# Dividing a softmax by its sums on ScalarE in place of GpSimd, in one attention stage of a two-layer decoder

## The chip, the cores and the metric

The kernel runs on one core of a Trainium2 chip. The metric is the device time of one execution in microseconds (us); the time of a kernel is the median of several runs. The engines are TensorE (PE in the profile; PEld is its loading of weights), VectorE (DVE), ScalarE (ACT), GpSimd (POOL) and SyncE (SP), which issues the DMAs.

## The reference

Two decoder layers work on 512 tokens of 1024 numbers in float32. Each layer is a SwiGLU feed-forward half-step, an attention and another half-step, all behind an RMS norm. The first layer's attention is "stick-breaking", the second's is sliding-window attention with 16 query heads of 64 and 2 key heads, and it is there that the change lies. Its softmax has one more term in the denominator, a learned "sink" of each head:

```python
m = jnp.maximum(jnp.max(scores, axis=-1, keepdims=True), sink)
p = jnp.exp(scores - m)
probs = p / (jnp.sum(p, axis=-1, keepdims=True) + jnp.exp(sink - m))
o = jnp.einsum('bnkgts,bnskd->bntkgd', probs.astype(v_band.dtype), v_band)
```

A block of 128 queries sees its own 128 keys and the 128 before it, behind a band mask; the first block has only its own.

## The kernel before

The program is a chain of stages: a feed-forward stage, the first attention, two feed-forward stages, the second attention (`sliding_window`, L1141) and a last feed-forward stage. Float32 products are made of three faster ones: a weight or an operand is split into a high half (a cast on ScalarE, in L345 for weights) and a low half (a subtraction, L350 on VectorE or L348 on GpSimd), and TensorE multiplies high by high, high by low and low by high (`terms`, L214).

TensorE's instructions keep the order in which the program issues them (class `_Ordered`, L75). ScalarE, VectorE (outside the first part of a feed-forward stage) and GpSimd get their order from the scheduler of the framework, which fills each engine's queue when the kernel is built, by priority and by when it reckons that an instruction can start; on the chip each queue is then worked off in that order. Semaphores are set by the framework from the tiles that an instruction reads and writes.

The second attention is cut into 16 turns: 4 chunks `c` of 4 heads, and in each 4 blocks `b` of 128 queries. In turn u (the loop of L1172) three things are interleaved:

- `window_scores` (L1045) of this turn: TensorE makes the scores `sc` of 4 heads (L1054 to L1059). VectorE adds the band mask and takes the row maxima in one instruction a head (L1067) and forms the shift of the exponent from the maxima and the sinks in three small ones (L1071 to L1073). This is the first part; in the next turn, ScalarE takes the exponent with the row sums, one Exp a head (L1076), and that of the sinks (L1080); VectorE adds the two (L1082) and takes the reciprocal (L1083); and GpSimd multiplies the whole tile `e` by the reciprocals, four heads in one instruction (L1084). A tile `e` is 128 x 4 x 256, in the first block of a chunk 128 x 4 x 128, and there are 4 buffers of it.
- `window_values` (L1088) of a turn three back: TensorE transposes `e` (`ptr`, L1100), ScalarE casts the result to a high half `ph` (L1103), VectorE subtracts to a low half `pl` (L1104), and TensorE multiplies both with the values (`pv`, L1112). ScalarE and VectorE split the product in the same way (`oh` L1113, `ol` L1114). The transposes have two PSUM buffers, shared with those of the queries (`qtr`, L1040), so a transpose waits until an earlier `ph` and `pl` have read theirs.
- Filling work for TensorE, a number of microseconds of it after each step (the lists WFILL and WRATE, L43 and L44): the products of the next chunk's queries (`tok`) and, later, those of the output matrix (`op`). The queries are squared on ScalarE (`qsq`, L1029), scaled on VectorE (L1030), given their rotary turn on GpSimd (L958 to L961), normalised on VectorE (`head_factor`, L963), transposed, and split by L644 on ScalarE and L645 on VectorE (`qs`).

The steps of a turn, cut to what matters:

```python
late = turning.pop(0) if u > 2 and turning else None
if scores:
    next(scores)               # the Exps of the turn before
...
if scores:
    next(scores)               # its sums, reciprocals and L1084
...
    scores = self.window_scores(c, b, turned[c], qs[c][0], e)
    turning.append(self.window_values(c, b, e, os, parts))
```

So a tile is normalised in the turn after its scores and transposed three turns after them.

Of the kernel before, what the change touches and what calls it, by code (L numbers as in the profile page):

```python
# [11 lines left out]
AF = mybir.ActivationFunctionType  # L12
# [3 lines left out]
P = 128  # L16
# [171 lines left out]
class _Trunk:  # L188
# [856 lines left out]
    def window_scores(self, c, b, qt, y, out):  # L1045

        nc, ap = self.nc, self.ap
        kh, kl = self.kt[c // 2]
        off = 0 if b else P
        ks = slice(max(b - 1, 0) * P, (b + 1) * P)  # L1050
        ts = slice(b * P, (b + 1) * P)
        z = self.psum.tile([P, 2, T], F32, tag="z", name="sc", bufs=1)
        z4 = z.rearrange("p q (i s) -> p q i s", i=2)
        for i in range(2):  # L1054
            for q in range(2):
                self.mm(z4[:, q, i, off:], qt[i][:, q, ts], kh[:, ks], start=True, stop=False)
            for q in range(2):
                rows = slice(q * HD, (q + 1) * HD)
                self.mm(z4[:, q, i, off:], qt[i][rows, q, ts], kl[rows, ks], start=False, stop=True)  # L1059
        yield  # L1060
        e = ap.tile([P, 4, 2 * P], F32, tag="e", name="e", bufs=4)
        st = ap.tile([P, 4, LINE // 4], F32, tag="st", name="st", bufs=4)[:, :, :4]
        f = y[:, 4 * b : 4 * b + 4]
        sink = self.sinks[:, 4 * c : 4 * c + 4]
        mx, neg, es, sm = (st[:, n, :] for n in range(4))
        for h in range(4):
            nc.vector.tensor_tensor_reduce(  # L1067
                e[:, h, off:], z4[:, h % 2, h // 2, off:], self.band[:, off:],
                scale=1.0, scalar=NEG, op0=ALU.add, op1=ALU.max, accum_out=mx[:, h : h + 1],
            )  # L1070
        nc.vector.scalar_tensor_tensor(mx, mx, -1.0, f, ALU.mult, ALU.mult)  # L1071
        nc.vector.scalar_tensor_tensor(neg, sink, -1.0, mx, ALU.mult, ALU.min)
        nc.vector.tensor_add(es, sink, neg)  # L1073
        yield
        for h in range(4):
            nc.scalar.activation(  # L1076
                e[:, h, off:], e[:, h, off:], AF.Exp, bias=neg[:, h : h + 1], scale=f[:, h : h + 1],
                accum_out=sm[:, h : h + 1],
            )
        nc.scalar.activation(es, es, AF.Exp)  # L1080
        yield
        nc.vector.tensor_add(sm, sm, es)  # L1082
        nc.vector.reciprocal(sm, sm)  # L1083
        nc.gpsimd.tensor_mul(e[:, :, off:], e[:, :, off:], sm[:, :, None].broadcast_to([P, 4, 2 * P - off]))  # L1084
        out.append(e)
        yield

# [223 lines left out]
```

## Time and profile before

| | us |
|---|---|
| median of 3 runs (1879.17 to 1884.75) | 1881.69 |
| the profiled execution's own time | 1884.44 |
| its span, first to last instruction | 1882.6 |
| TensorE busy (97% of the span) | 1834.2 |
| VectorE busy (80%) | 1500.1 |
| ScalarE busy (50%) | 938.1 |
| GpSimd busy (9%) | 170.2 |

The mean granted clock of TensorE over the execution is 0.985 of 2.4 GHz. The second attention lies at about 1340 to 1510 us of the span, its 16 turns at 1380 to 1503. In a timeline a row gives start, duration, engine, line, operation, output and inputs, shapes and count; in brackets stands how long the engine was idle before and what ended that. The line L85 is a helper's through which TensorE's instructions pass; it is told apart by the names of the tiles. "Granted clock" is the share of full speed at which TensorE was let run.

### The profile page before, as it was taken

The page shows a single profiled execution, that of the slowest core. Times are in us where ns is not written, and L with a number is a line of the kernel's source. Part 1 is how long each engine was busy: PE and PEld are TensorE (multiplying, and loading weights), DVE is VectorE, ACT ScalarE, POOL GpSimd, SP SyncE. Part 2 cuts the span into 40 slices and gives each one's busy share as a digit, 9 for nine tenths or more (in the row PEclk, how much of TensorE's full clock was granted, in tenths as well). Part 3 has the DMA queues.
Part 4 walks back from the last instruction along what each step waited for, and adds up shares of the span by engine and source line. Part 5 has one row for each costly group of instructions (what it writes and reads, how often), then busy time and mean ns, then how long its engine had stood idle before and what let it go on. Part 6 is the DMA issues. An engine that isn't in the chain of part 4 may idle for free.

```text
span 1882.6 us, 29285 instructions
## 1 busy us (share of the span) xinstructions
PE 1834.2 (97%) x11730; PEld 1651.1 (88%) x11730; DVE 1500.1 (80%) x2426; ACT 938.1 (50%) x1497; POOL 170.2 (9%) x131
## 2 busy tenths in 40 slices
PE   7999999999999999999999999999999899999999
PEld 5999999878787789999988999999887788999998
DVE  8888888668886988878768888787678588888884
ACT  6444444465664644444446444444356564444441
POOL 1000000333230100000010000000242210000000
PEclk8999999999999999999999999999989899999999
DMA  4333333221121423333323323322211043233331
GB/s 168 101 101 101 101 104 99 69 78 57 57 68 34 134 83 98 105 109 97 106 68 123 101 90 105 119 88 92 73 58 33 12 134 101 95 108 101 102 101 57
DMA packets 48809, 170.95 MB, mean 91 GB/s; under 512 B 5792, under 2 KB 6048, under 8 KB 48672
## 3 DMA queue, kind: packets, MB, share of 16 engines
q1 hardware_dynamic: 48672, 169.07, 28.2%
q8 instruction: 92, 1.51, 0.3%
q14 instruction: 45, 0.37, 0.1%
HBM read 166.96 MB, written 2.10 MB: 90 GB/s over the span
## 4 chain that ended last, share of the span: by engine, by line
PE 80%; DVE 11%; ACT 4%; issue 3%; POOL 1%; DMA 0%; SPq 0%; ACTq 0%; DVEq 0%; POOLq 0%
PE dn L85 25%; PE a L85 23%; PE c L85 11%; PE b L85 6%; PE gu L85 4%; PE tok L85 3%; PE op L85 3%; DVE keep L732 2%; PE pv L85 1%; DVE beta L733 1%; DVE t L85 1%; DVE qs L645 1%; PE sc L85 1%; DVE wt L755 1%; ACT keep L726 1%
## 5 line engine op out<-in xcount | busy, mean ns | idle before, releaser
L85 PE MATMUL dn<-hs,slot 128*128 128x512 f32 x1152 | 279.1, 391 | 0.0
L85 PEld LDWEIGHTS dn<-hs,slot 128*128 128x128 f32 x1152 | 211.0, 188 | 40.4
L85 PE MATMUL dn<-hs,slotx 128*128 128x512 f32 x960 | 234.2, 392 | 2.2 <-DVE hs L85 1.3
L345 ACT CAST slot<-raw 128x1024 fp32r<-128x1024 f32 (+1 forms) x155 | 160.0, 1033 | 145.1 <-PE a L85 55.2
L85 PE MATMUL a<-t,slot 128*128 128x256 f32 x1728 | 230.2, 283 | 0.0
L85 PEld LDWEIGHTS a<-t,slot 128*128 128x128 f32 x1728 | 222.7, 191 | 6.6
L85 PEld LDWEIGHTS dn<-hs,slotx 128*128 128x128 f32 x960 | 175.4, 188 | 37.5 <-DVE hs L85 2.2
L474 DVE SCALAR_TENSOR_TENSOR x<-dn,x 128x512 f32<-128x512 f32 x192 | 131.5, 685 | 44.9 <-PE dn L85 44.8
L350 DVE TENSOR_TENSOR slot<-raw,slot 128x1024 fp32r<-128x1024 f32 (+1 forms) x117 | 143.8, 1231 | 9.9 <-ACT slot L345 9.9
L85 PEld LDWEIGHTS a<-t,slotx 128*128 128x128 f32 x1008 | 131.0, 191 | 5.3
L85 PE MATMUL a<-t,slotx 128*128 128x256 f32 x1008 | 134.1, 283 | 0.0
L348 POOL TENSOR_TENSOR slot<-raw,slot 128x512 fp32r<-128x512 f32 x60 | 87.6, 1485 | 477.4 <-ACT slot L345 473.4
L85 PE MATMUL b<-xh,half 128*128 128x256 f32 x608 | 121.8, 283 | 0.0
L441 POOL TENSOR_TENSOR acc<-acc,sq 128x512 f32<-128x512 f32 x30 | 44.3, 1476 | 804.3 <-ACT sq L440 804.3
L85 PE MATMUL tok<-slot,xh 128*128 128x256 f32 x576 | 113.6, 296 | 0.1
L85 PEld LDWEIGHTS b<-xh,half 128*128 128x128 f32 x608 | 100.3, 192 | 0.0
L345 ACT CAST slotx<-raw 128x1024 fp32r<-128x1024 f32 x64 | 66.8, 1050 | 66.4 <-PE a L85 56.7
L345 ACT CAST slot<-rawx 128x1024 fp32r<-128x1024 f32 x60 | 63.1, 1052 | 69.7 <-PE a L85 43.6
L85 PE MATMUL c<-xh,slot 128*128 128x256 f32 x480 | 96.2, 283 | 0.0
L85 PEld LDWEIGHTS tok<-slot,xh 128*128 128x128 f32 x576 | 92.2, 197 | 3.3 <-issue 1.3
L553 DVE TENSOR_TENSOR g<-c,r 128x256 f32<-128x256 f32 x76 | 32.2, 424 | 75.8 <-PE c L85 75.6
L85 PE MATMUL gu<-xh,slot 128*128 128x512 f32 x256 | 87.3, 412 | 3.8 <-ACT xh L432 1.7
(360 smaller groups left out, 4216.7 us busy)
## 6 DMA issues: line engine op xcount, KB each, us to landing
raw<-in_w_dram SPq DMA_DIRECT2D x165, 512.0 KB, 3.5
rawx<-in_w_dram SPq DMA_DIRECT2D x96, 512.0 KB, 3.5
raw<-in_sbqk_dram SPq DMA_DIRECT2D x16, 512.0 KB, 3.4
raw<-in_swin_dram SPq DMA_DIRECT2D x10, 512.0 KB, 3.5
raw<-in_sbv_dram SPq DMA_DIRECT2D x8, 512.0 KB, 3.4
raw<-in_sbo_dram SPq DMA_DIRECT2D x8, 512.0 KB, 3.4
raw<-in_swo_dram SPq DMA_DIRECT2D x8, 512.0 KB, 3.4
x<-in_xt_dram SPq DMA_DIRECT2D x8, 256.0 KB, 5.4
```

The costliest lines, as they stand in the source:

```text
L85: return self._tc.keep_in_program_order(method(*args, **kwargs))
L345: nc.scalar.copy(hi, src)
L348: nc.gpsimd.tensor_sub(lo[:, h], src[:, h], hi[:, h])
L350: nc.vector.tensor_sub(lo, src, hi)
L441: (nc.gpsimd if k < POOL_SQUARES else nc.vector).tensor_add(self.acc, self.acc, sq)
L474: self.nc.vector.scalar_tensor_tensor(self.x[n], ps, factor, self.x[n], ALU.mult, ALU.add)
L553: nc.vector.tensor_add(g[:, W2:], ps, self.cells["r6", f])
L645: nc.vector.tensor_sub(out[other, h, :], src[own, :], out[own, h, :])
L726: nc.scalar.activation(keep[:, :, :n], z[:, :, :n], AF.Sigmoid, scale=-0.125)
L732: nc.vector.tensor_tensor_scan(rev, rev, rev, 1.0, ALU.mult, ALU.bypass)
L733: nc.vector.tensor_mul(beta[:, :, : n - 1], beta[:, :, : n - 1], keep[:, :, 1:n])
L755: nc.vector.tensor_sub(lo, src, hi)
```

## The change

The one instruction on GpSimd that multiplies the whole tile `e` by its four columns of reciprocals is replaced by four on ScalarE, one a head, each a Copy with the head's column as its scale. Result and place in the program stay the same. The diff in full:

```diff
@@ -1081,7 +1081,8 @@
         yield
         nc.vector.tensor_add(sm, sm, es)
         nc.vector.reciprocal(sm, sm)
-        nc.gpsimd.tensor_mul(e[:, :, off:], e[:, :, off:], sm[:, :, None].broadcast_to([P, 4, 2 * P - off]))
+        for h in range(4):
+            nc.scalar.activation(e[:, h, off:], e[:, h, off:], AF.Copy, scale=sm[:, h : h + 1])
         out.append(e)
         yield
```

## Rows read from the trace of the kernel before

**Rows 1.** The page's head and its part on busy time.

```profile
span 1882.6 us, 29285 instructions
PE 1834.2 (97%) x11730; PEld 1651.1 (88%) x11730; DVE 1500.1 (80%) x2426; ACT 938.1 (50%) x1497; POOL 170.2 (9%) x131
```

**Rows 2.** Windows: length; PE, PEld, DVE, ACT, POOL busy; PE's granted clock; DMA.

```profile
1380.00:1503.00 123.00, 109.26 (x697) 94.44 (x696) 91.24 (x322) 76.21 (x216) 41.03 (x34) 0.92 0.10 31
1464.00:1470.00 6.00, 5.86 (x23) 5.10 (x24) 3.24 (x16) 3.72 (x14) 1.89 (x1) 0.50 0.01 3
1483.00:1488.00 5.00, 4.02 (x15) 3.62 (x16) 3.38 (x17) 4.58 (x17) 1.77 (x2) 0.66 0.01 3
```

**Rows 3.** Timeline of TensorE, second attention: what it did after six waits.

```profile
1405.28 0.82 PE L85 MATMUL ptr<-ident,e 128*128 128x128 f32 x4 [1.95 <-DVE pl L1104]
...
1435.52 0.66 PE L85 MATMUL ptr<-ident,e 128*128 128x128 f32 x4 [1.55 <-DVE pl L1104]
...
1441.54 0.38 PE L85 MATMUL pv<-pl,v 128*128 128x256 f32 x1 [0.83 <-DVE pl L1104]
...
1457.47 0.66 PE L85 MATMUL qtr<-ident,q 128*128 128x128 f32 x4 [1.61 <-DVE pl L1104]
...
1464.14 1.12 PE L85 MATMUL ptr<-ident,e 128*128 128x128 f32 x4 [3.48 <-DVE pl L1104]
...
1483.98 0.46 PE L85 MATMUL pv<-pl,v 128*128 128x256 f32 x1 [1.34 <-DVE pl L1104]
```

**Rows 4.** Timeline of VectorE, second attention.

```profile
1401.18 0.17 DVE L1083 RECIPROCAL st<-st 128x4 f32<-128x4 f32 x1
...
1431.91 1.51 DVE L1071 SCALAR_TENSOR_TENSOR st<-st,hf 128x4 f32<-128x4 f32 x1
...
1438.31 2.57 DVE L350 TENSOR_TENSOR slot<-raw,slot 128x1024 fp32r<-128x1024 f32 x1
...
1441.40 1.21 DVE L350 TENSOR_TENSOR slot<-raw,slot 128x1024 fp32r<-128x1024 f32 x1
...
1455.07 1.34 DVE L1071 SCALAR_TENSOR_TENSOR st<-st,hf 128x4 f32<-128x4 f32 x1
...
1461.80 1.28 DVE L1072 SCALAR_TENSOR_TENSOR st<-line,st 128x4 f32<-128x4 f32 x1
...
1481.47 1.85 DVE L1072 SCALAR_TENSOR_TENSOR st<-line,st 128x4 f32<-128x4 f32 x1
...
1485.60 0.16 DVE L1072 SCALAR_TENSOR_TENSOR st<-line,st 128x4 f32<-128x4 f32 x1
```

**Rows 5.** Timeline of GpSimd, second attention.

```profile
1403.35 2.50 POOL L348 TENSOR_TENSOR slot<-raw,slot 128x512 fp32r<-128x512 f32 x2
...
1431.51 1.90 POOL L1084 TENSOR_TENSOR e<-e,st 128x1024 f32<-128x1024 f32 x1 [6.20 <-ACT qs L644]
...
1481.41 1.89 POOL L1084 TENSOR_TENSOR e<-e,st 128x1024 f32<-128x1024 f32 x1 [9.08 <-DVE st L1083]
```

**Rows 6.** Groups by line and form, 1380 to 1503 us.

```profile
L1084 POOL TENSOR_TENSOR e<-e,st 128x1024 f32<-128x1024 f32 x12 | 22.7, 1895 | 49.4 <-DVE st L1083 30.6 <-ACT qs L644 6.2 <-DVE st L1071 4.8
```

**Rows 7.** Timeline of ScalarE, behind the stage and in the next one.

```profile
1505.81 0.72 ACT L432 ACTIVATE xh<-x,gain 128x512 fp32r<-128x512 f32 x1
...
1539.36 1.29 ACT L468 ACTIVATE dg<-ident,nr 128x128 f32<-128x128 f32 x4 [1.20 <-DVE nr L85]
1540.55 1.94 ACT L506 ACTIVATE xg<-x,gain 128x512 f32<-128x512 f32 x3
```

**Rows 8.** Waits, total us, times, longest; and two rows of ScalarE's timeline.

```profile
ACT oh L1113 <- PE pv L85: 17.5, 9, 3.7
ACT e L1076 <- DVE st L1072: 15.1, 8, 3.9
...
1404.66 0.60 ACT L1076 ACTIVATE e<-e,st,hf 128x256 f32<-128x256 f32 x1 [0.81 <-DVE st L1072]
...
1468.58 0.50 ACT L1076 ACTIVATE e<-e,st,hf 128x128 f32<-128x128 f32 x1 [2.25 <-DVE st L1072]
```

## The prediction, made before the changed kernel was run

> **What bounds the kernel now.** I read the page's head first. TensorE is busy for 97% of the span [rows 1], so the time can change by what TensorE loses: the gaps in its stream and the stretches in which its clock is down. Both lie thick in the second attention stage. From the first Exp's band step to the last value product, 1380 to 1503 us, the windows view gives TensorE 109.3 us busy of 123, at a mean granted clock of 0.92 (of 2.4 GHz), VectorE 91.2, ScalarE 76.2 and GpSimd 41.0 [rows 2]. So 13.7 us are gaps and about 10 us (8% of 123) go to the clock, some 24 us in all; and no engine is full all the time: what is late is the order in which they hand work on.
>
> Which gaps? The timeline of TensorE shows six waits of over 0.8 us for `pl` (L1104), the longest of 3.48 [rows 3]. `pl` is one of VectorE's, and what stands ahead of it in VectorE's queue is stretched: L1071 and L1072 work on 128x4 values and take 0.16 us when nothing is in the way, yet 1.51, 1.34, 1.28 and 1.85 us just before four of these waits, and a slot's low half (L350) takes 2.57 us in place of 1.21 before a fifth [rows 4]. Beside each of the five runs a normalisation on GpSimd (L1084): the last began at 1481.41 for 1.89 us, and L1072, from 1481.47, ends at 1483.32, 0.02 us after it; the first pair, 1431.51 and 1431.91, ends in the same way [rows 4, 5]. GpSimd holds VectorE up where both read two operands in SBUF; nobody waits for the normalised tile itself, since by the code a tile is transposed two turns after it is normalised.
>
> After the wait of 3.48 us the granted clock is 0.50 over the next 6 us, that is 1.2 GHz, and 0.66 over the 5 us about the last wait [rows 2].
>
> **The change part by part.**
>
> *Removed: 16 normalisations on GpSimd.* Twelve take 1.9 us [rows 6]; the four of the first blocks have half the elements. GpSimd's own time is off the path and worth nothing, and behind these 16 its queue has only low halves of slots (L348) and the rotary products of the queries, which come earlier; no other queue, SP's included, loses an instruction. What counts is that VectorE is no longer held. Over the five stretched instructions that is 1.51-0.16 = 1.35, 2.57-1.21 = 1.36, 1.18, 1.12 and 1.69 us, 6.7 in all. TensorE gets at most its wait back: min(1.55, 1.35) + min(0.83, 1.36) + min(1.61, 1.18) + min(3.48, 1.12) + min(1.34, 1.69) = 1.35+0.83+1.18+1.12+1.34 = 5.8 us [rows 3, 4]. The sixth wait, at 1405.28, I don't credit: the low halves of a slot (L348) stood behind L1084 on GpSimd and ran from 1403.35 for 2.50 us [rows 5]; freed, they start earlier and hold VectorE in their turn. The Trainium skill (SBUF — State Buffer, "Who interferes with whom") says that of a VectorE instruction with two SBUF inputs and a GpSimd one that reads SBUF the second to issue is fully blocked, whatever the GpSimd one computes; by that rule the L348 pair goes on blocking, and the trace agrees (L1072 ends with L1084).
>
> *The clock.* Where the wait at 1483.98 goes, the clock after it should stay up: 0.34 of 5 us, 1.7 us [rows 2]. TensorE has hardly a gap behind it, so this counts in full. After 1464 the loss is 0.50 of 6 us, 3.0, but 3.48-1.12 = 2.4 us of that wait remain, and I credit nothing. Gain taken: 5.8 + 1.7 = 7.5 us. Bounds: 0 if all is given back, and 8.8 (the five waits whole) + 4.7 (both clock losses) = 13.5.
>
> *Added: 64 copies on ScalarE.* The trace has no copy of 128x256 from SBUF to SBUF with a scale column, but it has its neighbours: four of 128x128 (L468) start 1.19 us before the next line, 0.30 each, and three of 128x512 (L506) take 1.94, at most 0.65 each [rows 7]. A third of the way between is 0.42 for 128x256. A turn's set is 4 x 0.42 = 1.7 us (1.2 in the first block of a chunk), and 48 x 0.42 + 16 x 0.30 = 25.0 us in all. Copy with a scale column needs no change of ScalarE's table: after the stage's last Exp, L432 runs one at 1505.81 with no load ahead of it [rows 7]. No DMA comes or goes.
>
> *What of it lies on the path.* A set waits for VectorE's reciprocal (L1083) and holds up what is queued behind it on ScalarE: the casts `ph`, `oh` and `qs` and the next turn's Exps. VectorE's `pl` and `ol` wait for these casts, and TensorE for `pl`. I laid each set against ScalarE's timeline from its reciprocal on. In 7 of the 16 turns ScalarE then stands idle long enough, or what the set pushes is not what is late (turn 11: idle 2.25 us before the Exps at 1468.58, and the set takes 1.7) [rows 8]. In the other 9 ScalarE is in the middle of casts: in turn 2 the reciprocal comes at 1401.18, and the only idle time until the next Exps is 0.81 us [rows 4, 8]. Bounds for these nine: nothing, if the order puts the sets behind the casts that are late; 9 x 1.7 = 15.3, if every push arrives at TensorE. I take turn 2's row, since the nine are like it: 1.7 - 0.81 = 0.89 us each, 8.0 us.
>
> *The sum.* 8.0 - 7.5 = +0.5 us against the profiled execution of 1884.4 us (span 1882.6, 1.8 around it). That execution stands 2.7 above the median of 1881.7, and I forecast against the median: **1882.2 us**. What a measurement of this kernel can tell from no change is about 0.3%, 5.6 us.
>
> **The rivals.**
>
> *ScalarE becomes the bound of the stage (slower).* It needs 76.2 + 25.0 = 101.2 us. Of its 46.8 us of idle time, 15.1 lie before Exps that wait for VectorE's L1072 [rows 8], and these the copies and the quicker VectorE can use up; the other 31.7 are waits for TensorE (17.5 of them before `oh` [rows 8]) and stay if the chain keeps its shape. Then the stage takes 101.2 + 31.7 = 132.9 us, 9.9 more: 1891.6 us. It decides from the point where a set is longer than the idle time of its turn, and 25.0 against 15.1 says that it is on the whole. Against it: part of the 17.5 us is idle too, and a set can lie there. The Trainium skill (Perfetto Trace Analysis, "Identifying the Most-Contended Engine") takes the engine of highest occupancy as the bottleneck; by that rule VectorE, the busier of the two now, would hand this over to ScalarE, and the stage would go as in this rival. The trace bears it out in part only: TensorE, not VectorE, is busiest, and yet it loses its time to VectorE's queue.
>
> *The held VectorE was the whole trouble (faster).* The sets fall into idle time, the five waits go (8.8 us) and with the last of them its clock loss (1.7): 10.5 us less, 1871.2. For it: ScalarE's idle time before Exps is caused by the very instructions that L1084 stretches. Against: in 9 of 16 turns a set does not fit, and ScalarE's casts would be late next.
>
> *The change hardly shows.* The order on ScalarE is the planner's, and it may put a set behind the next turn's Exps; the tile still comes in time, as it is used two turns later, and VectorE is still held by what is left on GpSimd. Then gains and losses both are small: 1881.7.
>
> **How the numbers follow.** Forecast 0.40 and the third rival 0.05 lie within 0.3%; ScalarE as the bound 0.32; the freed VectorE 0.23. So faster 0.23, same 0.45, slower 0.32. The cases to both sides hold more than half of the chance; the forecast's own range is 1876 to 1888, the 5.6 us about it. The range takes the faster rival whole (1871) and reaches above the slower one by the 3.0 and 1.7 us of clock that longer waits could cost: 1891.6 + 4.7 = 1896, and a little for the bound of 15.3: 1871 to 1897.
>
> **What would show it.** Right: L1071 and L1072 back to 0.16 us everywhere but beside L348 and the rotary products; the waits for `pl` at turns 6, 7 and 13 gone or short; sets of four copies of about 1.7 us on ScalarE, busy for some 100 us in the stage; new waits of VectorE for `ph` and `oh`. Wrong: the copies take more than 0.5 us each, start to start; or ScalarE's busy share in the stage passes 85% and TensorE's waits end on `ph` or on Exps; or the waits for `pl` go and none come in their place; or the mean clock of the stage leaves 0.92 by more than 0.03, either way.

## The result, and the profile after

The changed kernel takes 1889.0 us (median of 11 runs, 1883.7 to 1892.3) where the kernel before takes 1879.6 in as many runs beside it. The ratio is 1.0048, with a 95% interval of 1.0033 to 1.0064: slower by 9.0 us (6.2 to 12.0), which is more than the 0.3% that a measurement can tell. 1889.0 lies inside the range that was given (1871 to 1897), but on the other side of 0.3% than the forecast of 1882.2, and outside the forecast's own 1876 to 1888.

First the page's head and its busy times, as [rows 1] before.

```profile
span 1887.4 us, 29286 instructions
PE 1836.0 (97%) x11730; PEld 1652.5 (88%) x11730; DVE 1491.3 (79%) x2426; ACT 960.3 (51%) x1561; POOL 143.3 (8%) x115
```

ScalarE has 22.2 us more, GpSimd 26.9 less, VectorE 8.8 less, in 64 more instructions on ScalarE and 16 fewer on GpSimd. Behind the changed line the line numbers are higher by one here (`pl` is L1105, `ph` L1104), and in the other runs they differ likewise; the names of the tiles tell the instructions apart. The windows (columns as in [rows 2]) say where it went.

```profile
1380.00:1503.00 123.00, 106.72 (x654) 92.13 (x653) 79.43 (x317) 94.49 (x274) 11.73 (x16) 0.89 0.10 31
1400.00:1410.00 10.00, 7.96 (x37) 7.23 (x36) 5.52 (x17) 8.86 (x22) 2.50 (x2) 0.50 0.17 52
1488.00:1493.00 5.00, 4.50 (x17) 3.92 (x18) 1.67 (x10) 4.48 (x15) 0.00 (x0) 0.66 0.00 0
```

In the same stretch as before VectorE is busy for 79.4 us in place of 91.2, ScalarE for 94.5 in place of 76.2; TensorE is busy for 2.5 us less, and its mean granted clock is 0.89 in place of 0.92. The stage itself can be measured between two events that every kernel here has: from TensorE's wait for the second turn's scores (`sc`, released by L1067) to its last wait, for `oh` in the first product `op`. Before, that is 1391.05 to 1502.95, with the waits of [rows 3] in between, 111.9 us; after, 1388.64 to 1507.69, 119.05: 7.2 us longer. Behind it both executions take 379.7 us. The two profiled executions differ by only 4.8 us as a whole, since that of before came to the stage 2.4 us later; so the stage's length, and not the span, is what to compare with the 9.0 us of the medians. The table below gives this length for every run.

The timeline of TensorE, its longest waits in the stage, against the six of [rows 3]:

```profile
1398.33 0.39 PE L85 MATMUL pv<-ph,v 128*128 128x256 f32 x1 [1.30 <-ACT ph L1104]
1404.22 1.09 PE L85 MATMUL ptr<-ident,e 128*128 128x128 f32 x4 [2.04 <-DVE qs L645]
1435.84 0.63 PE L85 MATMUL ptr<-ident,e 128*128 128x128 f32 x4 [1.11 <-DVE qs L645]
1453.01 0.63 PE L85 MATMUL qtr<-ident,q 128*128 128x128 f32 x4 [2.33 <-DVE st L1083]
1459.97 0.63 PE L85 MATMUL qtr<-ident,q 128*128 128x128 f32 x4 [1.69 <-DVE qs L645]
1480.56 0.39 PE L85 MATMUL pv<-ph,v 128*128 128x256 f32 x1 [1.20 <-ACT ph L1104]
1488.48 0.55 PE L85 MATMUL pv<-ph,v 128*128 128x256 f32 x1 [2.06 <-DVE st L1083]
```

All six waits of over 0.8 us for `pl` are gone; none for it is over 0.65. Seven others stand in their place. Five end on `ph` and `qs`, ScalarE's casts and what VectorE makes of them. Two are put down to L1083, but the instructions that wait need PSUM buffers that `pl` (at 1453.01) and `ol` (at 1488.48) read, and these stand just ahead of L1083 in VectorE's queue: before the last wait `oh` was ready at 1486.11, and `ol` came only at 1487.92, behind four masks (L1067). Not all of this is new: the waits that end on `qs` stand before the same transposes as three waits for `pl` of before (2.04, 1.11 and 1.69 us in place of 1.95, 1.55 and 1.61), three stand where before there was no wait of 0.5 us, and the last (2.06) one product ahead of the 1.34 us of before. The stage's waits of 0.2 us and more add up to 16.5 us, before to 13.4. The clock falls behind waits as before: it is 0.50 from 1400 to 1410 us, behind the wait of 1.30 us and around that of 2.04.

VectorE's small instructions, by line (count: shortest, median, longest ns, first and last start), against [rows 4]:

```profile
L1071 DVE SCALAR_TENSOR_TENSOR st<-st,hf x16: 131/161/484, 1383.4 to 1488.9; 128x4 f32<-128x4 f32 x16
L1072 DVE SCALAR_TENSOR_TENSOR st<-line,st x16: 133/161/165, 1383.9 to 1489.1; 128x4 f32<-128x4 f32 x16
```

So VectorE is free again: 1.85 us has become at most 0.17 for L1072, and the one L1071 of 0.48 stands at the stage's beginning, where before one of 0.48 stood too. The copies, by line and form, and VectorE's waits for ScalarE:

```profile
L1085 ACT ACTIVATE e<-e,st 128x256 f32<-128x256 f32 x48 | 20.5, 503 | 4.3 <-DVE st L1083 3.4 <-DVE st L1071 0.6 <-ACT qs L644 0.3
L1085 ACT ACTIVATE e<-e,st 128x128 f32<-128x128 f32 x16 | 5.1, 396 | 1.3 <-DVE st L1083 1.2
```

```profile
DVE qs L645 <- ACT qs L644: 8.1, 8, 1.7
DVE ol L1115 <- ACT oh L1114: 7.0, 7, 1.9
DVE pl L1105 <- ACT ph L1104: 5.9, 8, 1.8
ACT e L1085 <- DVE st L1083: 4.6, 4, 1.9
ACT e L1076 <- DVE st L1072: 3.9, 1, 3.9
```

The copies take 25.6 us, as worked out (25.0). ScalarE's waits before the Exps, 15.1 us before [rows 8], are down to 3.9. New is VectorE's waiting for `qs`: 8.1 us, where before it was 2.2. One place, on ScalarE's timeline:

```profile
1397.69 0.58 ACT L1104 CAST ph<-ptr 128x512 fp32r<-128x512 f32 x1
1398.17 1.71 ACT L1085 ACTIVATE e<-e,st 128x256 f32<-128x256 f32 x4
1399.78 0.37 ACT L1029 ACTIVATE qsq<-tok 128x256 f32<-128x256 f32 x1
1400.05 1.04 ACT L345 CAST slot<-raw 128x1024 fp32r<-128x1024 f32 x1
1400.98 0.58 ACT L644 CAST qs<-qtr 64x512 fp32r<-64x512 f32 x1
...
1402.77 0.58 ACT L644 CAST qs<-qtr 64x512 fp32r<-64x512 f32 x1
```

A set of copies stands ahead of the casts, then come two Exps (left out) and only then the second `qs`; VectorE's L645 waits for it, and TensorE, whose `ptr` needs the PSUM buffer that L645 reads, for L645: the 2.04 us at 1404.22. Two things are in this picture, the 1.7 us of the set and the order (two Exps ahead of a cast that TensorE waits for), and the experiments are about which of them costs.

### The profile page after: what moved, and what is told of

The parts are those of the page before. It is cut to its first block, busy times and chain, and to the rows that moved or that the text cites. A ratio compares the mean times of both kernels' runs of the same rounds, so it can differ in the third digit from the quotient of the medians.

```text
span 1887.4 us, 29286 instructions
## 1 busy us (share of the span) xinstructions
PE 1836.0 (97%) x11730; PEld 1652.5 (88%) x11730; DVE 1491.3 (79%) x2426; ACT 960.3 (51%) x1561; POOL 143.3 (8%) x115
## 4 chain that ended last, share of the span: by engine, by line
PE 81%; DVE 10%; ACT 5%; issue 3%; POOL 1%; DMA 0%; SPq 0%; ACTq 0%; DVEq 0%; POOLq 0%
PE dn L85 25%; PE a L85 23%; PE c L85 11%; PE b L85 6%; PE gu L85 4%; PE tok L85 3%; PE op L85 3%; DVE keep L732 2%; PE pv L85 2%; DVE beta L733 1%; PE sc L85 1%; DVE t L85 1%; PE q L85 1%; DVE wt L755 1%; DVE qs L645 1%
## 5 line engine op out<-in xcount | busy, mean ns | idle before, releaser
L350 DVE TENSOR_TENSOR slot<-raw,slot 128x1024 fp32r<-128x1024 f32 (+1 forms) x117 | 142.5, 1220 | 10.2 <-ACT slot L345 10.2
```

The costliest lines, as they stand in the source:

```text
L350: nc.vector.tensor_sub(lo, src, hi)
```

## The experiments

Two theories above all. By the first, **ScalarE's time** costs: 25 us more on an engine that the chain passes through. By the second, **the order** costs: the planner (the scheduler of the framework), which sees 64 more instructions, puts ScalarE's casts behind other work. Beside them stand smaller ones: the wait of a set for the reciprocal, and the place of the set. What the freed VectorE is worth is measured on its own.

| run | ratio to before | 95% interval | us | stage, us |
|---|---|---|---|---|
| the change | 1.0048 | 1.0033 to 1.0064 | +9.0 | 119.1 |
| no multiplication | 0.9941 | 0.9924 to 0.9959 | -11.1 | 100.2 |
| both: GpSimd's and 64 copies | 1.0031 | 1.0018 to 1.0043 | +5.8 | 116.1 |
| copies at the turn's end | 1.0027 | 1.0012 to 1.0042 | +5.1 | 115.9 |
| copies without the reciprocal | 1.0035 | 1.0022 to 1.0049 | +6.6 | 115.3 |
| copies for two heads | 1.0009 | 0.9996 to 1.0023 | +1.7 | 111.7 |
| 64 copies of 4 columns | 1.0003 | 0.9993 to 1.0013 | +0.6 | 108.5 |
| 16 copies of 4 columns | 0.9995 | 0.9982 to 1.0009 | -0.9 | 107.5 |
| the change, order held | 1.0011 | 0.9999 to 1.0022 | +2.1 | 111.3 |
| four on VectorE | 1.0013 | 1.0003 to 1.0023 | +2.4 | 111.0 |
| four on GpSimd, scalar column | 0.9949 | 0.9933 to 0.9966 | -9.6 | 103.9 |
| four on GpSimd, two tensors | 0.9956 | 0.9939 to 0.9973 | -8.3 | 102.4 |
| scalar column, last chunk shared | 0.9969 | 0.9956 to 0.9982 | -5.8 | 107.6 |

(us: ratio less 1, times the median of before beside it, 1879.6 to 1880.7; the stage before is 111.9 long. A stage's length is of one profiled execution each.)

### What the multiplication on GpSimd cost

**Left out.**

```diff
-        nc.gpsimd.tensor_mul(e[:, :, off:], e[:, :, off:], sm[:, :, None].broadcast_to([P, 4, 2 * P - off]))
```

> The multiplication of the tile by its reciprocal sums is left out altogether, so the softmax is not divided by its sums. The order of the instructions on ScalarE and VectorE is that of the kernel before, so this shows what VectorE gains when GpSimd no longer holds it, and nothing else. Theory A (freeing VectorE is worth 5.8 us of waits and 1.7 us of clock, and the changed kernel loses more than that on ScalarE): 5 to 10 us faster than before, about 1872; L1071 and L1072 at 0.16 us, the five waits for pl gone or short. Rival C (what VectorE gains is lost again in the next wait): within 3 us of before.

It takes 11.1 us less, a little more than theory A had, and ScalarE and VectorE have their instructions in the same order as before. The windows view, the stretch of [rows 2], and from TensorE's timeline the two waits for `pl` that are left:

```profile
1380.00:1503.00 123.00, 115.03 (x726) 98.37 (x725) 91.48 (x322) 84.25 (x229) 13.52 (x15) 0.97 0.13 41
```

```profile
1397.06 0.66 PE L85 MATMUL ptr<-ident,e 128*128 128x128 f32 x4 [1.69 <-DVE pl L1103]
...
1448.77 0.82 PE L85 MATMUL ptr<-ident,e 128*128 128x128 f32 x4 [2.36 <-DVE pl L1103]
```

The clock is 0.97, and TensorE is busy for 5.8 us more of the stretch. Of the six waits for `pl` two are left, before the same transposes as those of 1.95 us (1405.28) and 3.48 us (1464.14): the first is the one that the prediction didn't credit, and of the second it left 2.4 us. So the 16 normalisations cost 11.1 us where they stood, more than the 7.5 credited and inside its bounds (0 to 13.5).

**Four instructions on GpSimd, one a head, each with a scalar column.**

```diff
-        nc.gpsimd.tensor_mul(e[:, :, off:], e[:, :, off:], sm[:, :, None].broadcast_to([P, 4, 2 * P - off]))
+        for h in range(4):
+            nc.gpsimd.tensor_scalar(e[:, h, off:], e[:, h, off:], sm[:, h : h + 1], None, ALU.mult)
```

> The multiplication stays on GpSimd, as four instructions of one head each with the head's column as a scalar, in place of one with a broadcast. The order on ScalarE and VectorE is that of before. Theory A, that VectorE is held for as long as one GpSimd instruction lasts: with a quarter of the length VectorE's L1071 and L1072 are held for about 0.5 us at most, and 3 to 6 us are won against before. If GpSimd's four take much longer than 1.9 us together, or hold VectorE one after the other: no gain, or a loss of some us.

This is 9.6 us faster than before, more than either case expected, and the fastest measured of the kernels that do the whole work: it beats both. ScalarE and VectorE keep the order of before here, and in the next run too. GpSimd is busier with it (a set takes 3.6 us in place of 1.9), and yet VectorE is hardly held. VectorE's and GpSimd's timelines, two places:

```profile
1443.15 0.16 DVE L1071 SCALAR_TENSOR_TENSOR st<-st,hf 128x4 f32<-128x4 f32 x1
1443.57 0.15 DVE L1072 SCALAR_TENSOR_TENSOR st<-line,st 128x4 f32<-128x4 f32 x1
1470.47 0.43 DVE L1072 SCALAR_TENSOR_TENSOR st<-line,st 128x4 f32<-128x4 f32 x1
```

```profile
1442.60 3.64 POOL L1085 TENSOR_SCALAR e<-e,st 128x256 f32<-128x256 f32 x4 [1.95 <-ACT oh L1114]
1467.71 10.89 POOL L1085 TENSOR_SCALAR e<-e,st 128x256 f32<-128x256 f32 x12 [8.11 <-DVE st L1083]
```

L1071 and L1072 start inside a set and take 0.16 and 0.15; of the 16 that lie beside such sets alone the longest takes 0.43, and their mean is 0.21 (before: seven beside L1084, mean 1.06). The second row of GpSimd shows the price: three sets in a row at the stage's end, 10.9 us, and behind them two waits of TensorE for `e` of 0.57 us.

**The same four pieces, but products of two tensors.**

```diff
+        for h in range(4):
+            nc.gpsimd.tensor_mul(e[:, h, off:], e[:, h, off:], sm[:, h : h + 1].broadcast_to([P, 2 * P - off]))
```

> Four instructions on GpSimd, one a head, as in the run that gained 9.6 us, but of the old kind: a product of two tensors, the second a column broadcast over the row. If VectorE is held because the GpSimd instruction reads two tensors (theory kind), small instructions of VectorE are stretched again beside it, each by at most one piece of some 0.5 us, and most of the gain goes: -4 to +2 us against before. If only the length of one instruction counts, since VectorE gets in between two pieces (theory length), the gain stays: -11 to -7 us, and no small instruction of VectorE takes over 0.6 us.

The gain stays (8.3 us, which the two intervals don't tell from 9.6), but the longest small instruction is 0.63, not under 0.6, and one view shows that both theories hold a part:

```profile
1448.24 2.33 POOL L1085 TENSOR_TENSOR e<-e,st 128x256 f32<-128x256 f32 x4 [2.48 <-ACT oh L1114]
```

```profile
1448.82 0.63 DVE L1071 SCALAR_TENSOR_TENSOR st<-st,hf 128x4 f32<-128x4 f32 x1
1449.70 0.31 DVE L1072 SCALAR_TENSOR_TENSOR st<-line,st 128x4 f32<-128x4 f32 x1
```

Beside pieces of some 0.6 us with two tensors L1071 and L1072 take 0.41 on the mean (11 of them, up to 0.63), beside pieces of 0.92 us with a scalar column 0.21. So the kind of instruction decides how much VectorE is held, and the length of a piece bounds for how long: pieces of a quarter are enough to get most of the gain back.

**The scalar column, with two of the four heads on VectorE in the last chunk**, against the three sets in a row.

```diff
+            if c == CHUNKS - 1 and h % 2:
+                nc.vector.tensor_scalar(e[:, h, off:], e[:, h, off:], sm[:, h : h + 1], None, ALU.mult)
+            else:
+                nc.gpsimd.tensor_scalar(e[:, h, off:], e[:, h, off:], sm[:, h : h + 1], None, ALU.mult)
```

> As the run with four instructions with a scalar column on GpSimd, but in the last chunk two of the four heads are done by VectorE, so that GpSimd's sets of 3.6 us don't pile up behind its wait at the end of the stage (three sets, 10.9 us, without a gap). If the piled up sets are what that kernel still loses, its waits of TensorE for e, 0.57 + 0.57 us, go and perhaps a little clock: -11 to -12.5 us against before. If VectorE's 8 more instructions of 0.35 us hold up pl and the shifts there, -9 to -6 us.

A miss: 5.8 us are left of the 9.6, just outside the worse of the two cases. TensorE has a new wait of 2.20 us at 1473.11, for `ph`, and on ScalarE the cast that it waits for (1472.49) stands behind two turns' Exps, where in the order of before it stands behind one's; why the planner puts it there isn't shown. The waits for `e` are gone, as expected. This points to the order, as the following runs do.

**All four on VectorE** (`nc.vector.tensor_scalar`, one a head):

> The multiplication on VectorE, one instruction a head with the head's column as a scalar. At the 0.33 us, start to start, of L1030 (128x256) that is some 19 us more on VectorE, of which the stage has 91 us now. If VectorE's queue is as tight as ScalarE's: 0 to 9 us slower than before. If these run faster than L1030, as both operands and result are in SBUF and only one is a tile: 0.2 us each, 11 us in all, and 2 to 7 us faster than before.

+2.4 us, inside the first case: a piece takes 0.35 us (longest 1.37), VectorE is busy for 98 of the stretch's 123 us, and the gain is spent.

### What the copies on ScalarE cost

**GpSimd's multiplication kept, and 64 copies beside it** from the mask into a spare tile, scaled by the same columns:

```diff
+        spare = ap.tile([P, 2 * P], BF16, tag="spare", name="spare", bufs=1)
+        for h in range(4):
+            nc.scalar.activation(spare[:, off:], self.band[:, off:], AF.Copy, scale=sm[:, h : h + 1])
```

> The kernel before, with GpSimd's multiplication kept, and 64 copies more on ScalarE of the same width, with the same scale columns, from a constant tile to a spare one that nobody reads (bfloat16, for want of room). Theory A: the price of the copies alone, without the gain: 7.5 us slower than the changed kernel, so 14 to 19 us slower than before. Rival C: as the changed kernel, 9 us slower than before. If the copies can wait without harm, as nobody waits for the spare tile: less than 9.

+5.8 us, a miss for theory A and for rival C: less than the change itself, though both loads are there. The third case holds (less than 9). That the two costs lie in part on the same turns would fit, but isn't shown. Nobody reads these copies, so the planner is free to put them elsewhere than the change's; for a price of the copies this run is therefore no measure.

**The copies issued at the end of the turn**, behind its scores (a further step of the generator, which the loop takes there):

```diff
         nc.vector.reciprocal(sm, sm)
+        yield
+        for h in range(4):
+            nc.scalar.activation(e[:, h, off:], e[:, h, off:], AF.Copy, scale=sm[:, h : h + 1])
```

> The changed kernel with its four copies issued later in the program, at the end of the turn, behind the casts of the values and of the queries. ScalarE has just as much to do. Theory A1 (it is the copies' place in the queue, ahead of ph and qs, that costs): half of the loss or more is given back, so at most 4 us slower than before, perhaps faster. Rival A2 (it is ScalarE's load, wherever the copies stand): 7 to 12 us slower than before, as the changed kernel.

**The copies scaled by `es`**, the sinks' exponents, which ScalarE makes itself: no wait for VectorE.

```diff
+            nc.scalar.activation(e[:, h, off:], e[:, h, off:], AF.Copy, scale=es[:, h : h + 1])
```

> The changed kernel, its four copies scaled by the exponents of the sinks, which ScalarE has just made itself, in place of the reciprocals, so that they do not wait for VectorE (the softmax is not divided by its sums). Theory L (ScalarE's time, 25 us more in one queue, is what costs): 6 to 12 us slower than before, as the changed kernel. Theory W (a set that stands at the head of the queue and waits for L1083 is what costs): at most 3 us slower than before.

+5.1 and +6.6 us against the change's +9.0: the place is worth some 4 us, the wait for the reciprocal some 2.4, but the intervals overlap with the change's, so neither is sure. The first lies between A1 and A2, the second speaks for theory L and against W. Neither brings the 20.1 us (9.0 + 11.1) that lie between the change and no multiplication.

**Copies for two of the four heads**, and **64 copies of four columns**:

```diff
-        for h in range(4):
+        for h in range(2):
```

> The changed kernel with the copies of two heads of four alone; the other two stay undivided. GpSimd does nothing here. Left out altogether, the multiplication gave 11 us; with all four heads on ScalarE it took 9. Theory L with a price in proportion: 1 us faster than before, between 4 faster and 2 slower. If ScalarE's idle time takes up the first half and the second is paid in full: 6 to 10 us faster. Theory W (it is each set's wait and not its length): 4 to 9 us slower.

```diff
+            nc.scalar.activation(e[:, h, off : off + 4], e[:, h, off : off + 4], AF.Copy, scale=sm[:, h : h + 1])
```

> The changed kernel with all 64 copies, each over 4 columns of its head alone (the rest stays undivided): the waits for L1083 stay, the copies take about 0.1 us each, start to start, some 6 us in all. Theory L: 6 to 10 us faster than before, not far from leaving the multiplication out. Theory W, or the order of the other instructions that the planner changes along with the copies: 0 to 9 us slower than before.

A copy of four columns is not nearly free. By line:

```profile
L1085 ACT ACTIVATE e<-e,st x64: 280/286/309, 1391.0 to 1485.8; 128x4 f32<-128x4 f32 x64
```

0.286 us each, against 0.503 for 256 columns: most of a copy's time does not depend on its size. Four take 0.86, in all 13.8 us, about what two heads' whole copies take (13.7). The two heads' +1.7 us lies at the slow end of what theory L gave; the small copies' +0.6 us lies in theory W's range, but theory L's figure rested on 0.1 us a copy, where it is 0.2 (0.86 for four). Against no multiplication the runs lose 11.7 us (small copies) and 12.8 us (two heads), the whole change (25.6 us of copies) 20.1. Up to here all this looks like ScalarE's time, at 0.8 to 0.9 us for each us.

**16 copies of four columns**, one a turn, tells time from order:

```diff
+        nc.scalar.activation(e[:, 0, off : off + 4], e[:, 0, off : off + 4], AF.Copy, scale=sm[:, 0:1])
```

> One copy of 4 columns of one head a turn in place of four, 16 in all (the rest is left undivided); by the 0.29 us of each this is 4.6 us of ScalarE's time, where the four a turn took 13.8. If the time on ScalarE is what costs (theory A), the gain of leaving the multiplication out, 11.1 us, is given back in proportion: 11.6 x 4.6/13.8 = 3.9 us, so -7 us against before (-9 to -5), ratio 0.995 to 0.997. If it is that ScalarE's queue waits for VectorE's reciprocal once a turn, or that the planner orders ScalarE and VectorE otherwise when a copy stands there (theory B), the time stays where it was with four: +0.5 us (-2 to +3).

-0.9 us: with a third of the time of the 64 small copies nearly their loss, 10.2 us against no multiplication where they lost 11.7. Time on ScalarE alone is out: it gave -9 to -5, and the interval is -3.4 to +1.7. ScalarE's timeline at the same place, first without the multiplication, then with the 16 copies:

```profile
1393.69 0.58 ACT L644 CAST qs<-qtr 64x512 fp32r<-64x512 f32 x1
1394.27 0.37 ACT L1112 CAST oh<-pv 128x256 fp32r<-128x256 f32 x1
1394.70 0.59 ACT L1102 CAST ph<-ptr 128x512 fp32r<-128x512 f32 x1
1395.31 0.58 ACT L644 CAST qs<-qtr 64x512 fp32r<-64x512 f32 x1
1396.44 0.60 ACT L1076 ACTIVATE e<-e,st,hf 128x256 f32<-128x256 f32 x1 [0.55 <-DVE st L1072]
```

```profile
1396.49 0.58 ACT L644 CAST qs<-qtr 64x512 fp32r<-64x512 f32 x1
1396.96 0.30 ACT L1084 ACTIVATE e<-e,st 128x4 f32<-128x4 f32 x1
1398.01 0.60 ACT L1076 ACTIVATE e<-e,st,hf 128x256 f32<-128x256 f32 x1 [0.74 <-DVE st L1072]
...
1399.31 0.58 ACT L644 CAST qs<-qtr 64x512 fp32r<-64x512 f32 x1
...
1401.31 0.37 ACT L1113 CAST oh<-pv 128x256 fp32r<-128x256 f32 x1
1401.58 0.59 ACT L1103 CAST ph<-ptr 128x512 fp32r<-128x512 f32 x1
```

Without it the order is `qs`, `oh`, `ph`, `qs`, four Exps. With one small copy it is `qs`, copy, two Exps, `qs`, two Exps, `oh`, `ph`: `oh` comes 4.8 us after the first `qs`, not 0.6. A copy of 0.3 us can't make that; another order in the queue does. TensorE's waits of this run end, like those of the change, on `qs` (2.45 and 1.18 us) and `ph` (1.20), and on `ol` (1.72), which here too comes behind VectorE's masks. The other half of theory B, the wait for the reciprocal, isn't out: before five of the 16 copies ScalarE stands idle for it, 4.5 us in all.

**The whole change with the order held.** All 64 copies, and all other instructions of ScalarE and VectorE held in their order of before; the copies are put between them by a list, where ScalarE stood idle in the run without the multiplication. The trace bears it out: without the copies, both engines' instructions come in the order of before.

```diff
+    def hold_order(self, traced):
...
+            line = [mine[k] if k >= 0 else self.copies[-k - 1] for k in order]
+            for first, then in zip(line, line[1:]):
+                self.tc.add_manual_dep(
+                    then, first.name,
+                    mybir.DependencyInfo(mybir.DependencyClass.NoSync, mybir.DependencyReason.DATA),
+                    reason="order",
+                )
```

> All 64 copies of the changed kernel, whole, with ScalarE's and VectorE's other instructions held in the order that they have in the kernel before (an issue order alone, no wait), and the copies put by hand between them, where ScalarE stood idle in the run without the multiplication, in time for the transposes. If the time on ScalarE is what costs (theory A), 25 us of copies cost here what they cost in the changed kernel: +5 to +10 us against before. If the order that the planner makes around a copy is what costs (theory B: casts for TensorE fall behind Exps), most of the gain of leaving the multiplication out, 11.1 us, stays: -4 to -11 us, and TensorE has no wait of 1 us or more that ends on qs, ph or ol. In between (-4 to +5), both have a part, and it is split by the number.

In between: +2.1 us (-0.2 to +4.1). The same 25 us of copies cost 13.2 us against no multiplication, and the planner's order and place the other 7.0 (9.0 - 2.1; by the two intervals 3 to 11); the stages give 11.1 and 7.7. The windows view, and TensorE's waits for ScalarE's casts and for `pl`:

```profile
1380.00:1503.00 123.00, 110.39 (x693) 94.07 (x692) 82.44 (x323) 98.10 (x279) 12.43 (x17) 0.93 0.10 31
```

```profile
1400.43 0.38 PE L106 MATMUL pv<-ph,v 128*128 128x256 f32 x1 [1.55 <-ACT ph L1125]
...
1404.87 0.66 PE L106 MATMUL ptr<-ident,e 128*128 128x128 f32 x4 [1.70 <-DVE pl L1126]
...
1461.86 1.12 PE L106 MATMUL ptr<-ident,e 128*128 128x128 f32 x4 [2.23 <-DVE pl L1126]
```

No wait of 1 us ends on `qs` or `ol` any more, one still ends on `ph`, and the clock is 0.93 in place of 0.89. The two waits for `pl` aren't owed to the copies: the same two transposes wait 1.69 and 2.36 us without the multiplication. New against that run are the 1.55 us for `ph`, 1.18 us for the scores at 1452.84 and 0.58 us at 1481.85 for a copy that I put too late, and the clock is 0.93 in place of 0.97. ScalarE is now busy for 98 of 123 us. So the 13.2 us are ScalarE's time together with what my placing leaves, and no run parts the two.

## Why the prediction was right or wrong

Between the two events that bound the stage TensorE has the same instructions in the same order in every run. This stretch in the windows view (columns as in [rows 2]): before, no multiplication, the change, the order held.

```profile
1391.05:1502.95 111.90, 99.54 (x624) 85.82 (x624) 81.84 (x283) 70.95 (x202) 33.43 (x26) 0.91 0.08 25
1384.54:1484.75 100.21, 93.63 (x624) 80.75 (x624) 71.93 (x283) 70.69 (x202) 7.13 (x10) 0.97 0.09 27
1388.64:1507.69 119.05, 103.39 (x623) 88.82 (x623) 72.89 (x283) 92.86 (x265) 7.11 (x10) 0.89 0.07 23
1389.29:1500.63 111.34, 100.13 (x623) 85.22 (x623) 72.57 (x283) 93.49 (x265) 7.15 (x10) 0.92 0.08 25
```

The length less TensorE's busy time gives the gaps: 12.4, 6.6, 15.7 and 11.2 us. As the instructions are the same, the busy time (99.5, 93.6, 103.4 and 100.1 us) differs with the granted clock. Each row is one execution.

- **What bounds the kernel**: right. The gaps and the clock in the stage are what moved: it is 7.2 us longer, of which 3.3 are gaps and 3.9 busy time at a lower clock.
- **The held VectorE**: the mechanism was right, L1072 is at 0.17 us or less everywhere. Without the multiplication the gaps fall by 5.8 us, just what was worked out, and 2.36 us of the longest wait stay, for which 2.4 were. What was too small is the clock: TensorE is busy for 5.9 us less where 1.7 were credited. Before, the clock was also 0.50 from 1406 to 1412 us, behind the wait of 1.95 us, which the prediction left out; at the same place without the multiplication (1397 to 1403) it is 1.00, though 1.69 us of that wait stay. So 7.5 was taken and 11.1 measured, inside the bounds.
- **The copies' own time**: right, 25.6 us against 25.0, a set 1.71 against 1.7.
- **"I take turn 2's row, since the nine are like it: 1.7 - 0.81 = 0.89 us each, 8.0 us"**, taken for the whole cost, is the step that failed. The copies cost 20.1 us (18.9 in the stage), beyond the bound of 15.3. Two things were left out. One is the clock: the sum has it on the side of the gain, and nothing for the clock behind the waits that the copies bring; only the range has 4.7 us of it. From no multiplication to the change the gaps grow by 9.1 us, near the 8.0, but the busy time grows by another 9.8, at a clock of 0.89 in place of 0.97. The other is the order: the set was laid against a ScalarE timeline that was taken to stay as it was, but the order on ScalarE and VectorE is made anew when the kernel is built. With the old order held and the copies placed by hand, 7.0 of the 20.1 us go, and no count of idle time could show these; casts that come to stand behind Exps (and `ol` behind masks) are what the traces show of them. The gaps then grow by 4.6 us and the busy time by 6.5. So that 8.0 lies near 9.1 is in part luck. The prediction named the planner's order only as something that could help.
- **The sum**: +0.5 forecast, +9.0 measured, with the gain too small by 3.6 us and the cost by 12.1. By the stage, the forecast had 2.2 us more of gaps and 1.7 us less for the clock; it got 3.3 more of gaps and 3.9 more for the clock. That 1889.0 lies in the range is owed to the slower rival, up to which the range was drawn, and not to the sum.
- **The rivals**: the slower one, ScalarE as the stage's bound, gave 9.9 us and is what came in sign and size. Its two numbers nearly hold: of the 15.1 us of waits before Exps 3.9 are left, and of the other 31.7 us of idle time some 29.3 (of the 130 us from 1380 to 1510 ScalarE is idle for 33.2, as it does 96.8). By the Trainium skill (Perfetto Trace Analysis, "Identifying the Most-Contended Engine") that role would have gone from VectorE to ScalarE; the trace agrees so far as ScalarE is the busier of the two now (94.5 to 79.4). But with the order held, ScalarE is just as busy and 7 us come back, so its load is not the whole of it, and the size of 9.9 is in part luck. The faster rival was right about what the freed VectorE is worth (10.5 against 11.1) and wrong that the sets fall into idle time.
- **What would show it**: right were the small instructions, the waits for `pl`, the sets, ScalarE's busy time and VectorE's new waits, though they are for `qs` more than for `ph` and `oh`. Of the marks against the forecast one came in half: TensorE's waits end on `ph`, at a ScalarE share of 77%, not 85; and the clock's fall from 0.92 to 0.89 stops just short of another.

What stays open is how the 13 us of the held order split between ScalarE's time and where I put the copies: no other placing was tried. Nor was the planner's order tried without any copy.

## What to carry to other kernels

Where a scheduler orders the queues, an added instruction costs its time and the order that it brings about: read the order of the new program first, and hold the old one (or put the instruction by hand) to see what it costs by itself. Where a wait brings the clock down, price the clock with the wait: here it was about half of the cost. An instruction that nobody waits for can still be the cost, by what it holds up; before it is moved to another engine, try it where it is in smaller pieces or in a form that holds less: here that gave 9.6 us faster where the move gave 9.0 us slower. And idle time of an engine that the chain passes through is not room to fill.

## What the runs showed of the hardware

- On GpSimd the form with a scalar column takes longer than a product of two tensors (0.92 us for 128x256 against some 0.6), and yet it holds VectorE's two-operand instructions hardly at all: 0.21 us on the mean beside it, 0.41 beside the other, 0.15 alone. The Trainium skill (SBUF — State Buffer, "Who interferes with whom") has a VectorE instruction with two inputs in SBUF contend with any GpSimd one that reads SBUF, and the later one fully blocked. L1072, which took 1.85 us beside L1084, agrees; L1072 at 1443.57, 0.15 us in the middle of a set of 3.64, does not, and there the measurement decides.
- A ScalarE copy of 4 columns takes 0.286 us, one of 256 columns 0.503. Cutting a copy short saves less than half of it.
